# The first stage of a two-layer hybrid encoder kernel: modulation blocks and norm tiles in a fixed order, state-space parameters and weight splits on the vector engine

## The chip, the cores and the metric

The kernel runs on one core of a Trainium2 chip. The metric is the device time of the whole program in microseconds, as the median of several executions. A core has a matrix engine (TensorE, PE in the profile), a vector engine (DVE), a scalar engine for activations and copies (ACT), GpSimd (POOL), and SyncE (SP), which issues most of the DMAs. Each runs its own queue of instructions in order, and semaphores tie the queues together. PEld is PE's loading of weights, which overlaps its matmuls.

## The reference

A trunk of two residual layers on x of 512 positions by 1024 channels, conditioned by a vector c. Only the first layer's mixer (layer 0) bears on the change:

```python
mod = (silu(c) @ ada_w[layer] + ada_b[layer])            # 6 x 1024
sh1, sc1, g1, sh2, sc2, g2 = split(mod, 6)
u = rms_norm(h, norm_w[layer, 0]) * (1.0 + sc1) + sh1
z = u @ hyb_w_in[e]                                      # 1024 -> 512 + 512 + 128 + 128
y_s5  = s5_mixer(z_s5, ...)                              # complex diagonal scan, both directions
y_att = axial_gqa(z_q, z_k, z_v, ...)                    # 8 query heads, 2 key heads, RMS norm and rotary
mix = concatenate([y_s5, y_att]) @ hyb_w_out[e]
h = h + g1 * mix                                         # then a squared-ReLU MLP, then layer 1
```

The state-space mixer turns its parameters into a magnitude exp(lr dt), an angle li dt with its sine and cosine, and complex factors f = (abar - 1) / lambda that scale its input matrices. These *parameters* are 128 x 32 numbers, worked on by many small operations. In the attention q and k are divided by the root mean square of each head, rotated, and q is scaled by 1/8 before the softmax.

## The kernel before

Matrix products run in three passes: each operand is split in a high and a low half (`wh`, `wl` for weights, `acta`, `actb` for activations), and `mm3_tok` adds high by high, low weight by high activation, and high weight by low activation. `split` (L504) makes a weight's halves: ACT copies the high half (L509), another engine subtracts it for the low half (L510).

`hybrid` (the program of the first layer, from L1100 on) runs in this order:

1. *First stage.* Eight tiles of x (128 channels x 512 positions) are loaded. `s5_params` makes the state-space parameters on POOL, through the class `Tiny`, which makes one scalar-tensor-tensor operation out of two of POOL's. `rope_tables` makes the four rotary tables `rcq`, `rsq`, `rck`, `rsk` on POOL. `rstd_bc` squares the x tiles on ACT, adds them on DVE, sums over the partitions on PE (L752), takes the reciprocal root on DVE (L731 to L736, result `nry`), broadcasts it on PE (L756) and copies it to SBUF on ACT (L757). The modulation of 1024 channels comes in four blocks of 256: `ada_load` fetches eight pieces of 128 x 512 and `ada_block` multiplies them by silu(c) and adds them on DVE (L712, L714), sums over the partitions on PE (L716) and adds the bias on DVE (L719, L720). Each block serves two of the eight tiles of x, called a pair here. `norm_tile` makes the normalised, modulated tile: DVE L763, ACT L766 (high half), DVE L767 (low half). PE then multiplies it with the q, k and v columns of the input weight (256 columns of k and v for each of four position blocks, 512 of q: L596 to L598). For k < 3 the low half of the weight tile is made by POOL, after that by DVE.
2. *State-space input and attention preparation.* `s5_tables` (L298 to L304) makes sine and cosine tables, `s5_in` the state-space columns of the projection for two halves, `s5_prep` (L342 to L346) and `s5_lag` (L415) the matrices of one unit of the loop: `PREP` puts preparation 2 on DVE and the others on POOL. `attn_kv` and `attn_q` take the sums of squares by head (`head_ss`: one ACT operation for each head), the reciprocal roots, and the rotation (two products from PSUM on DVE, an addition on POOL). POOL scales the queries (L942) and takes their low halves. The first gate accumulations of `ada_half` (L670, 128 x 512 pieces fetched by ACT's queue into two buffers `nt`) follow on DVE.
3. *The loop.* Eight units of the state-space mixer: phases, the products L441 to L443, the scans L448 on DVE, between them steps of the attention (row maximum on DVE, exponential on ACT, products on PE), and the preparations of later units.
4. *The tail.* Once the last scan is done, the GELU (L1047), the gate, the output projection, the MLP and the second layer follow. PE's order in them is written out by hand; they are the same lines before and after.

What sets the order on an engine is the tile framework's scheduler, which takes instructions as their operands become ready by its reckoning; `issue_after(i)` keeps what stands in its block behind instruction i, and `manual_schedule` fixes PE's order in the tail. Tiles come from pools with a number of buffers for each name: a new tile waits for the readers of the one that it replaces. `weights(wctx, 3, 3, 768)` gives the weight tiles of the first stage three buffers for the raw weight and three for the halves.

## Time and profile before

| | |
|---|---|
| three runs | 1259.51, 1261.17, 1262.28 us, median 1261.17 |
| the profiled execution | 1262.24 us, of which the span of the trace is 1260.4 |
| mean granted clock of PE | 0.973 |
| busy in the span | PE 1174.1 us (93%), PEld 997.9 (79%), DVE 820.2 (65%), ACT 527.5 (42%), POOL 244.9 (19%) |
| the chain of work that ended last | PE 71%, DVE 15%, POOL 8%, issue 3%, ACT 3% |

Times in a trace count from the start of the span. The rows below cut the span at points of the program. At 27.4 PE's first matmul of a norm tile starts; at 42.5 the second operand that it needed is there; at 73.2 DVE ends the norm steps of the fourth pair; at 118.5 DVE begins to feed the loop's first products; at 250.3 the last scan is over. An engine's busy time in a stretch is set against the length of the stretch. PEclk is the TensorE clock granted in the stretch, as a share of 2.4 GHz, so 0.50 is 1.2 GHz. In the timeline a row can stand for several instructions (xcount) from its start on; in square brackets is how long the engine sat idle before, and what released it. Of a single line the duration is given as smallest, median and largest of its instructions.

### The profile page before, as it was taken

The numbers are of one execution on the slowest core, as the hardware profiler recorded it, in microseconds if no ns is written. First come the engines' busy times: TensorE is split into PE (matmuls) and PEld (weight loads), VectorE is DVE, ScalarE is ACT, GpSimd is POOL, SyncE is SP. The second block draws the span as 40 slices with busy tenths as digits, with TensorE's granted clock in tenths as the row PEclk, the third lists the DMA queues.
The fourth block names the chain that finished last, engine by engine and source line by source line (L and its number), as shares of the span: only waits on it lengthen the run. The fifth ranks groups of instructions, "written<-read, shape, count | busy, mean of one in ns | idle before, by whom it ended". The sixth has DMA issues, their size and how long they took to land.

```text
span 1260.4 us, 17174 instructions
## 1 busy us (share of the span) xinstructions
PE 1174.1 (93%) x6552; PEld 997.9 (79%) x6552; DVE 820.2 (65%) x1246; ACT 527.5 (42%) x954; POOL 244.9 (19%) x342
## 2 busy tenths in 40 slices
PE   3678889989999999999999999789999999999997
PEld 2568668777998888888888988569988888888887
DVE  6558999977789875678533779995753322445143
ACT  3147658545352342134422449853543321334130
POOL 9996987520000000000000053000000000000000
PEclk9989889999999999999999999789999999999998
DMA  9421311054538855667332332112242333222311
GB/s 335 129 59 56 88 43 34 2 180 156 200 103 272 274 187 200 216 196 244 112 100 84 101 109 76 50 57 78 69 126 91 101 101 100 91 93 101 101 34 67
DMA packets 83858, 151.76 MB, mean 120 GB/s; under 512 B 5696, under 2 KB 30272, under 8 KB 83776
## 3 DMA queue, kind: packets, MB, share of 16 engines
q1 hardware_dynamic: 75712, 137.04, 33.4%
q10 hardware_dynamic: 8064, 13.64, 3.4%
q8 instruction: 51, 0.84, 0.3%
q14 instruction: 31, 0.25, 0.1%
HBM read 148.55 MB, written 2.10 MB: 120 GB/s over the span
## 4 chain that ended last, share of the span: by engine, by line
PE 71%; DVE 15%; POOL 8%; issue 3%; ACT 3%; DMA 0%; DVEq 0%; ACTq 0%; POOLq 0%
PE ps L557 12%; PE ps L558 12%; PE ps L556 12%; PE px L556 8%; PE px L557 8%; PE px L558 8%; DVE actb L448 2%; DVE wl L510 2%; PE po L984 1%; POOL tiny L77 1%; DVE actb L443 1%; DVE s5m L442 1%; DVE actb L441 1%; DVE nb L966 1%; DVE ti L1404 1%
## 5 line engine op out<-in xcount | busy, mean ns | idle before, releaser
L510 DVE TENSOR_TENSOR wl<-wr,wh 128x1024 fp32r<-128x1024 f32 (+2 forms) x175 | 211.3, 1209 | 288.5 <-ACT wh L509 277.9
L509 ACT CAST wh<-wr 128x1024 fp32r<-128x1024 f32 (+2 forms) x170 | 173.3, 1023 | 437.3 <-PE ps L557 203.6
L557 PE MATMUL ps<-actb,wh 128*128 128x512 f32 (+1 forms) x512 | 181.1, 354 | 0.1
L556 PE MATMUL ps<-acta,wh 128*128 128x512 f32 (+1 forms) x328 | 116.5, 356 | 0.0
L558 PE MATMUL ps<-acta,wl 128*128 128x512 f32 (+1 forms) x328 | 115.9, 354 | 0.0
L556 PE MATMUL ps<-hid,wh 128*128 128x512 f32 x288 | 112.1, 389 | 0.0
L558 PE MATMUL ps<-hid,wl 128*128 128x512 f32 x288 | 112.0, 389 | 0.0
L557 PE MATMUL ps<-hid,wh 128*128 128x512 f32 x288 | 112.0, 389 | 0.0
L557 PEld LDWEIGHTS ps<-actb,wh 128*128 128x128 f32 x512 | 97.5, 190 | 13.5 <-DVE actb L846 0.3
L556 PE MATMUL px<-hid,wh 128*128 128x512 f32 (+1 forms) x288 | 98.9, 343 | 0.0
L557 PE MATMUL px<-hid,wh 128*128 128x512 f32 (+1 forms) x288 | 98.4, 342 | 0.0
L558 PE MATMUL px<-hid,wl 128*128 128x512 f32 (+1 forms) x288 | 98.4, 342 | 0.0
L557 PE MATMUL px<-actb,wh 128*128 128x512 f32 (+1 forms) x224 | 85.5, 382 | 0.0
L638 DVE SCALAR_TENSOR_TENSOR acc<-wr,cact,acc 128x1024 f32<-128x1024 f32 x49 | 62.9, 1284 | 18.7 <-DMA wr<-ada_w 18.3
L556 PEld LDWEIGHTS ps<-acta,wh 128*128 128x128 f32 x328 | 62.7, 191 | 8.5
L558 PEld LDWEIGHTS ps<-acta,wl 128*128 128x128 f32 x328 | 62.6, 191 | 8.4
L1331 POOL MEMSET xp<- 128x2 f32 x8 | 0.7, 98 | 351.6 <-PE px L558 347.3
L556 PE MATMUL ps<-actc,wh 128*128 128x512 f32 (+1 forms) x184 | 65.1, 354 | 0.0
L558 PE MATMUL ps<-actc,wl 128*128 128x512 f32 (+1 forms) x184 | 64.8, 352 | 0.0
L556 PEld LDWEIGHTS ps<-hid,wh 128*128 128x128 f32 x288 | 54.1, 188 | 11.3
L558 PEld LDWEIGHTS ps<-hid,wl 128*128 128x128 f32 x288 | 54.1, 188 | 11.2
L557 PEld LDWEIGHTS ps<-hid,wh 128*128 128x128 f32 x288 | 54.1, 188 | 11.1
(495 smaller groups left out, 2758.4 us busy)
## 6 DMA issues: line engine op xcount, KB each, us to landing
wr<-w SPq DMA_DIRECT2D x128, 512.0 KB, 3.7
wr<-ada_w SPq DMA_DIRECT2D x56, 512.0 KB, 4.5
wr<-wout SPq DMA_DIRECT2D x16, 512.0 KB, 3.5
araw<-ada_w ACTq DMA_DIRECT2D x32, 256.0 KB, 3.4
wr<-win SPq DMA_DIRECT2D x16, 512.0 KB, 3.9
acta<-ada_w SPq DMA_DIRECT2D x16, 256.0 KB, 5.4
actb<-ada_w SPq DMA_DIRECT2D x16, 256.0 KB, 5.4
nt<-ada_w ACTq DMA_DIRECT2D x16, 256.0 KB, 2.8
```

The lines of the kernel that those rows point to most:

```text
L77: self.eng.tensor_scalar(t, a, s, None, op0=op0)
L441: V.tensor_tensor(v[:, xs, dst], er[:, xs], p1[:, :, src], op=ALU.mult)
L442: V.tensor_tensor(m, ei[:, xs], p2[:, :, src], op=ALU.mult)
L443: V.tensor_tensor(v[:, xs, dst], v[:, xs, dst], m, op=op)
L448: self.scan = V.tensor_tensor_scan(vv, m4, vv, 0.0, op0=ALU.mult, op1=ALU.add)
L509: nc.scalar.copy(hi, src)
L510: (lo_eng or nc.vector).tensor_tensor(lo, src, hi.bitcast(F32), op=ALU.subtract)
L556: mm(out, wh, xh, start=first and a == a0 and lead(o), stop=False, skip_group_check=True)
L557: mm(out, wh, xl, start=False, stop=False, skip_group_check=True)
L558: mm(out, wl, xh, start=False, stop=last and a == a0 + kk - 1, skip_group_check=True)
L638: nc.vector.scalar_tensor_tensor(acc, raw, self.ca[:, k:k + 1], acc, op0=ALU.mult, op1=ALU.add)
L966: nc.vector.reduce_max(nb, s, axis=AX.X, negate=True)
```

## The change

The class `Tiny` goes, and the parameter operations of `s5_params` run on the vector engine. The function becomes a generator with two parts: the first, up to the magnitude exp(lr dt), stands ahead of `rstd_bc` in the program, the second is issued behind the last norm tile, together with the rope tables, which also go to the vector engine, and `s5_tables`.

All low halves of weights in the first stage are made by the vector engine. The weight tiles of the stage have four raw buffers in place of three. `ada_load` puts the pieces of blocks 0 and 1 in the activation buffers as before, those of block 2 in the buffers that later hold the rotated queries (`qr0` to `qr3`), those of block 3 in the buffers of the keys and of two attention tiles. Each modulation block, and the splits of the two weight tiles that go with it, are held behind the low halves (and for the splits also the high half) of the pair of norm tiles before. In block 0 the four odd pieces are not accumulated on DVE but multiplied by silu(c) on PE, four one-column matmuls each (L714 of the new kernel). All four blocks write to one PSUM bank. `rstd_bc` returns the broadcast in PSUM, without the copy to SBUF.

`head_ss` takes one ACT operation for the squares of all heads and one sum over them on DVE. The scale of the queries is no longer multiplied into them: POOL's four products go, and the softmax's exponential takes the scale of its rows as its own, with a scaled row maximum from one more one-column ACT operation for each of the 32 steps.

```diff
@@ s5_params
-        V = D = Tiny(self, tp, nc.gpsimd)
+        V = D = nc.vector
...
         reduce(r, t("rn"))
+        mag = pexp(x)
+        yield
...
-        mag = pexp(x)
...
+        yield
@@ wtile
-    def wtile(self, src, pool=None):
+    def wtile(self, src, pool=None, after=()):
...
-        self.split(hi, lo, raw, self.hi_eng, self.lo_eng)
+        with self.behind(*after):
+            self.split(hi, lo, raw, self.hi_eng, self.lo_eng)
@@ ada_load
-            raw = self.tl(self.ap, "actb" if k % 2 else "acta", [P, 2, 256], bufs=8)
+            if cb < 2:
+                raw = self.tl(self.ap, "actb" if k % 2 else "acta", [P, 2, 256], bufs=8)
+            elif cb == 2:
+                if k % 2 == 0:
+                    pair = hp.tile([P, 4, 256], F32, tag=f"qr{k // 2}", name=f"raw{k // 2}")
+                raw = pair[:, k % 2 * 2:k % 2 * 2 + 2]
+            elif k < 4:
+                raw = hp.tile([P, 2, 256], F32, tag=("kth0", "ktl0", "kth1", "ktl1")[k], name=f"rawk{k}")
+            else:
+                raw = self.tl(qp, ("pts", "q2")[k % 2], [P, 2, 256], bufs=2)
@@ ada_block
+            if k in direct:
+                for i in range(4):
+                    nc.tensor.matmul(ps[:, i:i + 1], flat[k][:, i * P:(i + 1) * P], self.ca[:, k:k + 1],
+                                     start=k == direct[0] and i == 0, stop=False, skip_group_check=True)
+            elif k == 0:
-            nc.tensor.matmul(ps[:, i:i + 1], acc[:, i * P:(i + 1) * P], self.ones, start=True, stop=True)
+            nc.tensor.matmul(ps[:, i:i + 1], acc[:, i * P:(i + 1) * P], self.ones, start=not direct and i == 0, stop=True, skip_group_check=True)
@@ rstd_bc
-        nc.scalar.copy(acc, bc)
-        return acc
+        return bc
@@ rope_tables
-                nc.gpsimd.tensor_tensor(o, self.col[tab].rearrange("p (t d) -> p t d", t=4),
+                nc.vector.tensor_tensor(o, self.col[tab].rearrange("p (t d) -> p t d", t=4),
@@ head_ss
-        for h in range(nh):
-            self.nc.scalar.activation(sq, ps[:, h * 64:(h + 1) * 64], AF.Square, accum_out=dst[:, h:h + 1])
+        self.nc.scalar.activation(sq, ps, AF.Square)
+        self.nc.vector.reduce_sum(dst, sq.rearrange("p (h d) -> p h d", h=nh), axis=AX.X)
@@ attn_q
-            nc.gpsimd.tensor_tensor(o[:, :, 0], o[:, :, 0], rq[:, t * 8:t * 8 + 8].unsqueeze(2).to_broadcast([P, 8, 64]), op=ALU.mult)
@@ the softmax step
-        self.exp = nc.scalar.activation(p, s, AF.Exp, bias=nb, accum_out=self.esum[:, h, t:t + 1])
+        r = self.rq[:, t * 8 + h:t * 8 + h + 1]
+        nc.scalar.activation(nb, nb, AF.Identity, scale=r)
+        self.exp = nc.scalar.activation(p, s, AF.Exp, bias=nb, scale=r, accum_out=self.esum[:, h, t:t + 1])
@@ hybrid
-        self.weights(wctx, 3, 3, 768)
+        self.weights(wctx, 4, 3, 768)
...
-        raws = [self.ada_load(aw, 0)]
-        self.lo_eng = nc.gpsimd
-        self.s5_params(sp, tp)
-        self.rope_tables(self.pool(wctx, "rope"))
-        xbc = self.rstd_bc(x, "ps")
+        raws = self.ada_load(aw, 0, hp, qp)
+        params = self.s5_params(sp, tp)
+        next(params)
...
+            cb, a = k // 2, k % 2
+            if a == 0:
+                with self.tc.issue_after(self.last.ins) if k else ExitStack():
+                    mods.append(self.ada_block(qp, raws, cb, psm[:, cb * 4:cb * 4 + 4], (1, 3, 5, 7) if cb == 0 else ()))
+                w += [self.wtile(win[i * P:(i + 1) * P, 512:1280], after=(self.last, self.last_hi) if k else ()) for i in (k, k + 1)]
+                if cb < 3:
+                    raws = self.ada_load(aw, cb + 1, hp, qp)
...
         with self.tc.issue_after(self.last.ins):
+            next(params)
+            self.rope_tables(self.pool(wctx, "rope"))
             self.s5_tables(sp, 0)
```

What stands where on the engines' queues changes in three places. The first is PE's opening, from the sum of the squares on. `ps<-ones,nacc` is that sum, `consts_sb,nry` the broadcast of the root, `ones,pexp` the end of a modulation block, and `wh`, `wl` with `acta`, `actb` the products of norm tiles. Before:

```order
L752 MATMUL ps_371<-ones,nacc_348 128x1 x4
L716 MATMUL p_95_397<-ones,pexp_398 128x1 x4
L756 MATMUL ps_385<-consts_sb,nry_377 128x128 x4
L596 MATMUL ps_395<-wh_448,acta_455 128x256
L596 MATMUL ps_396<-wh_448,acta_455 128x256
L596 MATMUL ps_391<-wh_448,acta_455 128x512
L596 MATMUL ps_392<-wh_448,acta_455 128x512
L596 MATMUL ps_393<-wh_448,acta_455 128x512
L596 MATMUL ps_394<-wh_448,acta_455 128x512
L716 MATMUL p_106_430<-ones,pexp_431 128x1 x4
L597 MATMUL ps_395<-wl_449,acta_455 128x256
L598 MATMUL ps_395<-wh_448,actb_456 128x256
```

After:

```order
L757 MATMUL ps_241<-ones,nacc_218 128x1 x4
L761 MATMUL p_49_255<-consts_sb,nry_247 128x128 x4
L714 MATMUL p_36_217<-cact,actb_150 128x1 x4
L714 MATMUL p_36_217<-cact,actb_154 128x1 x4
L714 MATMUL p_36_217<-cact,actb_158 128x1 x4
L714 MATMUL p_36_217<-cact,actb_162 128x1 x4
L721 MATMUL p_36_217<-ones,pexp_266 128x1 x4
L588 MATMUL ps_264<-wh_295,acta_324 128x256
L589 MATMUL ps_264<-wl_296,acta_324 128x256
L588 MATMUL ps_265<-wh_295,acta_324 128x256
L589 MATMUL ps_265<-wl_296,acta_324 128x256
L588 MATMUL ps_260<-wh_295,acta_324 128x512
```

The group of the second modulation block (`pexp_431`) stood among the first tile's products and now stands behind both tiles of its pair; the sixteen direct products of block 0 stand behind the broadcast of the root, and the first low-half products follow each high one at once.

The second is DVE's queue around the last pair of norm tiles. `modb` is the modulation, `nt` the normalised tile, `wl` the low half of a weight, the `sm_`, `s5mt`, `s5pi` and `s5npr` tiles are parameters, `s5si` and `s5co` the tables of `s5_tables`. Before:

```order
L720 SCALAR_TENSOR_TENSOR modb_154_654<-modb_154_654,cols_sb 128x2
L763 SCALAR_TENSOR_TENSOR nt_735<-h_144,modb_154_654,nacc_348 128x512
L763 SCALAR_TENSOR_TENSOR nt_771<-h_146,modb_154_654,nacc_348 128x512
L767 SCALAR_TENSOR_TENSOR actb_738<-nt_735,modb_154_654,acta_737 128x512
L767 SCALAR_TENSOR_TENSOR actb_774<-nt_771,modb_154_654,acta_773 128x512
L298 SCALAR_TENSOR_TENSOR s5si_802<-sm_phi_204,consts_sb 128x512 x2
L510 TENSOR_TENSOR wl_767<-wr_765,wh_766 128x768
L302 TENSOR_SCALAR s5co_801<-s5si_802 128x1024
L303 SCALAR_TENSOR_TENSOR s5si_802<-s5co_801,s5si_802 128x1024
L304 SCALAR_TENSOR_TENSOR s5co_801<-s5si_802 128x1024
```

After:

```order
L767 SCALAR_TENSOR_TENSOR nt_614<-h_144,modb_111_599,p_49_255 128x512
L767 SCALAR_TENSOR_TENSOR nt_644<-h_146,modb_111_599,p_49_255 128x512
L771 SCALAR_TENSOR_TENSOR actb_617<-nt_614,modb_111_599,acta_616 128x512
L771 SCALAR_TENSOR_TENSOR actb_647<-nt_644,modb_111_599,acta_646 128x512
L212 TENSOR_TENSOR s5pi_676<-sm_phi_188,consts_sb 128x80 x2
L215 MEMSET s5mt_674 128x160
L220 TENSOR_TENSOR sm_m_129_694<-pexp_34_200 128x32
L241 TENSOR_TENSOR sm_den_715<-sm_lr_164 128x32
L242 TENSOR_TENSOR sm_ta_716<-cols_sb 128x32
L884 TENSOR_TENSOR rcq<-consts_sb,cols_sb 128x256
L884 TENSOR_TENSOR rsq<-consts_sb,cols_sb 128x256
L884 TENSOR_TENSOR rck<-consts_sb,cols_sb 128x256
```

The tables of `s5_tables` and the low halves for the state-space columns followed the norm tiles at once; now the second part of the parameters and the rope tables stand between, and the tables come behind them.

The third is POOL's queue where the first two preparations stand. `sm_` tiles are parameters again, `s5cv`, `s5vr`, `s5vi` and `s5ptmp` belong to `s5_prep`, `qr` is a rotated query and `actb` a buffer of the loop's products. Before:

```order
L342 TENSOR_TENSOR s5cv_206_958<-s5pr_220,s5par_946 128x320
L342 TENSOR_TENSOR s5cv_207_959<-s5npr_222,s5par_946 128x320
L256 TENSOR_SCALAR sm_nr_301<-sm_ar_295 128x32
L262 TENSOR_TENSOR sm_ta_303<-sm_ai_296,cols_sb 128x32
L265 TENSOR_TENSOR sm_fi_305<-sm_ai_296,sm_lr_164 128x32
L261 TENSOR_TENSOR sm_fr_304<-sm_nr_301,sm_lr_164 128x32
L263 TENSOR_TENSOR sm_fr_304<-sm_fr_304,sm_ta_303 128x32
L264 TENSOR_TENSOR sm_fr_304<-sm_fr_304,sm_den_302 128x32
```

After:

```order
L390 TENSOR_TENSOR s5dd_952<-consts_sb,cols_sb 128x256
L1220 TENSOR_TENSOR sel<-consts_sb 128x32
L327 TENSOR_TENSOR s5cv_169_918<-s5pr_675,s5par_906 128x320
L327 TENSOR_TENSOR s5cv_170_919<-s5npr_677,s5par_906 128x320
L898 TENSOR_TENSOR qr_1083<-qr_1083,tmp_1084 128x8x64
L943 TENSOR_TENSOR qr_1083<-qr_1083 128x8x64
L898 TENSOR_TENSOR qr_1093<-qr_1093,tmp_1094 128x8x64
L898 TENSOR_TENSOR qr_1103<-qr_1103,tmp_1104 128x8x64
L943 TENSOR_TENSOR qr_1093<-qr_1093 128x8x64
L414 MEMSET actb_1353 128x4
L414 MEMSET actb_1354 128x4
L445 MEMSET actb_1400 128x4
```

POOL went from the parameters to the preparations; now nothing of the parameters stands on it, and the preparations' other operations (`s5vr`, `s5vi`, `s5ptmp`) stand behind the first rotations of the queries and fillings of the loop's buffers, a few rows further on.

## Rows read from the trace of the kernel before

**Rows 1.** Busy time of each engine by stretch, with granted clock and DMA.

```profile
0.00:42.50 42.50, 9.65 (x38) 8.80 (x38) 27.66 (x51) 13.52 (x20) 38.58 (x70) 1.00 0.69 248
42.50:73.20 30.70, 24.84 (x126) 22.04 (x127) 17.53 (x29) 9.61 (x23) 27.97 (x48) 0.83 0.47 150
73.20:118.50 45.30, 41.65 (x311) 37.56 (x310) 32.12 (x69) 29.27 (x129) 34.43 (x47) 0.96 0.20 57
118.50:250.30 131.80, 118.23 (x970) 96.61 (x969) 126.78 (x238) 81.64 (x185) 100.94 (x129) 0.94 0.15 44
250.30:1260.40 1010.10, 979.77 (x5114) 832.88 (x5113) 616.12 (x863) 393.50 (x597) 42.93 (x51) 0.98 0.39 127
```

**Rows 2.** PE's waits up to 300 us: us in total, times, longest.

```profile
PE ps L597 <- POOL wl L510: 11.1, 1, 11.1
```

**Rows 3.** Timeline: start, us, engine, line, operation, tiles, count, idle before.

```profile
21.15 0.20 DVE L736 SCALAR_TENSOR_TENSOR nry<-nra,nry 128x4 f32<-128x4 f32 x1
...
23.01 2.06 PE L756 MATMUL ps<-consts_sb,nry 128*128 128x128 f32 x8
29.73 1.70 PE L716 MATMUL p<-ones,pexp 128*128 128x1 f32 x8
...
32.65 1.39 ACT L766 ACTIVATE acta<-nt,modb 128x512 fp32r<-128x512 f32 x2 [3.20 <-DVE nt L763]
...
60.56 0.94 PE L716 MATMUL p<-ones,pexp 128*128 128x1 f32 x8
67.34 0.58 PE L596 MATMUL ps<-wh,acta 128*128 128x256 f32 x1 [5.83 <-ACT acta L766]
...
78.41 0.28 PE L596 MATMUL ps<-wh,acta 128*128 128x256 f32 x1
...
82.59 0.28 PE L596 MATMUL ps<-wh,acta 128*128 128x256 f32 x1
```

**Rows 4.** Busy time and granted clock of the two microseconds from 71.0.

```profile
71.00:73.00 2.00, 2.00 (x9) 1.81 (x8) 1.87 (x3) 1.36 (x2) 1.92 (x5) 0.50 0.45 130
```

**Rows 5.** Single lines: smallest, median, largest ns; first and last start in us.

```profile
L1513 DVE SCALAR_TENSOR_TENSOR lp_p<-lp_p,lp_w x6: 174/174/176, 453.2 to 454.2; 128x16 f32<-128x16 f32 x6
...
L714 DVE SCALAR_TENSOR_TENSOR pexp<-acta,cact,pexp x12: 741/752/797, 16.2 to 57.9; 128x512 f32<-128x512 f32 x12
...
L448 DVE TENSOR_TENSOR_SCAN actb<-s5m,actb x64: 391/466/1485, 133.1 to 248.8; 128x128 f32<-128x128 f32 x64
...
L670 DVE SCALAR_TENSOR_TENSOR h<-nt,cact,h x14: 721/1150/1723, 119.4 to 178.4; 128x512 f32<-128x512 f32 x14
```

**Rows 6.** DVE's groups up to 262 us: busy us, mean ns, idle before.

```profile
L448 DVE TENSOR_TENSOR_SCAN actb<-s5m,actb 128x128 f32<-128x128 f32 x64 | 42.2, 706 | 0.0
L443 DVE TENSOR_TENSOR actb<-actb,s5m 128x254 f32<-128x254 f32 x32 | 22.3, 718 | 0.0
L442 DVE TENSOR_TENSOR s5m<-s5ei,pb 128x254 f32<-128x254 f32 x32 | 12.9, 403 | 0.0
...
L510 DVE TENSOR_TENSOR wl<-wr,wh 128x768 fp32r<-128x768 f32 x5 | 5.0, 1005 | 6.5 <-ACT wh L509 6.4
```

**Rows 7.** Timeline of ACT, DVE and POOL from 94 to 251 us.

```profile
94.82 1.28 ACT L732 ACT_TABLE_LOAD   x1
...
97.23 0.37 DVE L344 TENSOR_TENSOR s5ptmp<-s5nfpi,s5par 128x256 f32<-128x256 f32 x1
...
117.01 1.63 DVE L415 SCALAR_TENSOR_TENSOR s5dc<-p,consts_sb,s5dc 128x64 f32<-128x64 f32 x4
...
118.03 4.68 POOL L942 TENSOR_TENSOR qr<-qr,rqy 128x512 f32<-128x512 f32 x4
...
125.68 1.60 DVE L670 SCALAR_TENSOR_TENSOR h<-nt,cact,h 128x512 f32<-128x512 f32 x1 [4.87 <-DMA nt<-ada_w]
...
250.19 2.33 DVE L1047 SCALAR_TENSOR_TENSOR nt<-nt,h 128x512 f32<-128x512 f32 x2
```

**Rows 8.** Busy time by engine while POOL runs preparations 0 and 1.

```profile
76.99:96.50 19.51, 17.22 (x100) 15.29 (x100) 8.30 (x15) 10.80 (x40) 19.03 (x26) 0.92 0.21 62
```

More of the change, by code (lines that the diff above doesn't have):

```diff
@@ L513, in wraw, with behind @@
         return self.tl(self.wp, "wr", [P, self.WC], bufs=self.WR)
-    def wtile(self, src, pool=None):
+    def behind(self, *ins):
+        st = ExitStack()
+        for i in ins:
+            st.enter_context(self.tc.issue_after(i.ins))
+        return st
+    def wtile(self, src, pool=None, after=()):
         nk, ncol = src.shape[0] // P, src.shape[1]
@@ L749, in rstd_bc @@
             nc.vector.tensor_tensor(acc, acc, sq, op=ALU.add)
-        ps = self.psum(tag)
+        ps = self.psum(tag[0])
         for t in range(4):
@@ L937, in attn_q @@
             self.qr.append(o)
-        rq = self.rsqrt(hp, ss.rearrange("p t h -> p (t h)"), 32, 64.0, "rq")
-        nc.vector.tensor_scalar(rq, rq, 0.125, None, op0=ALU.mult)
-        for t in range(4):
-            o = self.qr[t]
-            nc.gpsimd.tensor_tensor(o[:, :, 0], o[:, :, 0], rq[:, t * 8:t * 8 + 8].unsqueeze(2).to_broadcast([P, 8, 64]), op=ALU.mult)
             nc.scalar.copy(o[:, :, 1].bitcast(F32R), o[:, :, 0])
             nc.gpsimd.tensor_tensor(o[:, :, 0], o[:, :, 0], o[:, :, 1], op=ALU.subtract)
+        self.rq = self.rsqrt(hp, ss.rearrange("p t h -> p (t h)"), 32, 64.0, "rq")
+        nc.vector.tensor_scalar(self.rq, self.rq, 0.125, None, op0=ALU.mult)
         self.esum = self.tl(hp, "esum", [P, 8, 4])
@@ L1123, in hybrid @@
             x.append(t)
-        raws = [self.ada_load(aw, 0)]
-        self.lo_eng = nc.gpsimd
-        self.s5_params(sp, tp)
-        self.rope_tables(self.pool(wctx, "rope"))
-        xbc = self.rstd_bc(x, "ps")
-        u = []
+        raws = self.ada_load(aw, 0, hp, qp)
+        params = self.s5_params(sp, tp)
+        next(params)
+        u, w, mods = [], [], []
+        psm = self.psum("p5")
+        xbc = self.rstd_bc(x, ("ps", "p5"))
         psq = [self.psum() for _ in range(4)]
         psk = [self.psum() for _ in range(2)]
-        mods = []
-        wt = lambda k: self.wtile(win[k * P:(k + 1) * P, 512:1280])
         for k in range(8):
-            if k % 2 == 0:
-                for cb in range(0 if k == 0 else k // 2 + 1, min(k // 2 + 2, 4)):
-                    if cb:
-                        raws.append(self.ada_load(aw, cb))
-                    mods.append(self.ada_block(qp, raws[cb], cb, self.psum("p5")))
-            m, a = mods[k // 2], k % 2
-            self.lo_eng = nc.gpsimd if k < 3 else None
-            wh, wl = wt(k)
+            cb, a = k // 2, k % 2
[5 more added lines that the diff above has]
+                    raws = self.ada_load(aw, cb + 1, hp, qp)
+            m = mods[cb]
+            wh, wl = w[k]
             xh, xl = self.norm_tile(x[k], xbc, m[:, 2 + a:3 + a], m[:, a:a + 1])
```

30 lines of the change are left out of this document (8 added, 22 removed).

## The prediction

> **What bounds the kernel now.** I read the table by stretches first [rows 1]. VectorE (DVE) is busy 126.78 of the 131.80 us from 118.5 to 250.3, the stretch with the state-space loop, and PE after 250.3 is busy 979.77 of 1010.10. So the kernel is a first part that ends with the last scan on DVE, and a tail in which PE is full. The tail is written in the same order after the change and begins behind that scan: what the change does is how far the scan's end moves. It stands at 250.2, where DVE goes on to the first GELU product [rows 7].
>
> Before 118.5 DVE is not full: busy 27.66, 17.53 and 32.12 in 42.5, 30.7 and 45.3 us, so 41 us idle, and 46 up to 250.3. GpSimd (POOL) is all but full there (38.58, 27.97, 34.43) with the parameter chain [rows 1]. PE stands still 11.1 us for the low half of a weight tile that POOL computes [rows 2]. The change takes these waits away and gives the work to DVE. The question is whether 46 us of DVE idle time shrink by more than DVE's work grows.
>
> **The change part by part, along DVE's queue.**
>
> *Opening.* Of the parameters 39 small operations now stand on DVE ahead of or among the seven additions of the squares and the square-root step. A dependent one of 16 columns takes 0.174 us and they follow every 0.2 (six starts in 1.0) [rows 5], so 7.8 us for 39; about 5 of them fit in before the activations land, and four of block 0's eight products at 0.75 [rows 5] leave. The reciprocal root, finished at 21.35 now [rows 3], I put at 22.8. PE then broadcasts it (2.06) and, in its queue behind that, multiplies half of block 0 directly: 16 matmuls, four times a group like the one of 8 passes that took 1.70 at 29.7 and 0.94 at 60.6 [rows 3], so 3.8 to 6.8, and the last group 0.94 to 1.70. From the end of such a group to the first matmul of a norm tile take 2.0 (the group at 29.73 ends 31.43, the high half of the first tile at 32.65 plus half of 1.39) [rows 3]. First weight matmul: 22.8 + 2.06 + 3.8 + 0.94 + 2.0 = 31.6, up to 35.4; I take 32.5. It starts at 27.4 now but then hangs till 42.5.
>
> *The four pairs.* A tile is 4.18 us of matmuls at full clock (82.59 less 78.41) [rows 3]. Each block's modulation group now stands behind the pair before on PE and the next norm tile waits for it: 8.36 + 0.94 + 2.0 = 11.3 per pair. DVE has seven or eight products (0.68 apart without POOL), two low halves (1.0 each) [rows 5, 6] and four norm steps, 10.3, so PE's chain sets the period. In the 2.0 us PE idles. After 5.83 us idle at 67.3 the granted clock is 0.50, that is 1.2 GHz, until about 73 [rows 3, 4], which costs 2.8 us of a pair. For a gap of 2.0 the price lies between 0 and 2.8; I take 1.0, since the gap is nearer to no gap than to 5.83. Period 12.3 (11.3 to 14.1), so the fourth pair's norm tiles come at 32.5 + 36.9 = 69.4 (65.5 to 77.7). In the trace of before DVE ends the fourth pair at 73.2, where the third stretch begins [rows 1]: nearly nothing is gained for DVE here, because the modulations wait for PE where POOL's split made PE wait before.
>
> *From there to the state-space factors.* DVE does 32.12 us from 73.2 to 118.5 now [rows 1]. Of it two weight halves come earlier and 20 operations of preparation 2 and of the lag blocks (0.27 to 0.66 each, from 97.2 to 118.5 [rows 7]) come later, in all 9.1. Added are the other 43 parameter operations at 0.2 to 0.33 (9.5), four rope tables of 256 columns (1.4, half a product of 512) and eight sums of squares by head (four of 512 columns, four of 128: 3.2); the contended ones get some 2 us shorter as POOL is quiet. 32.1 - 9.1 + 14.1 - 2 = 35. ScalarE (ACT) alternates here between sine and square root, two more table loads at 1.28 [rows 7], for which DVE waits about 2. So the factors and the query scale are ready 1.5 + 35 + 2 = 38.5 after the fourth pair, at 107.9. Now POOL is done with both preparations by 96.5 [rows 8].
>
> *The gate accumulations.* DVE's next rows are the products of the early gate blocks. They read two buffers that ACT's queue refills, and ACT now has phase copies, exponentials and preparation copies ahead of the refills. One such wait was 4.87 [rows 7]. There are about ten refills in this stretch; I take 8 us of waits, bounds 5 and 12.
>
> *The loop.* 126.8 of work now, plus the 20 operations (7.4) and three more attention maxima that come ahead of the last scan (2.4): 136.6. Beside it POOL now has preparations 0 and 1, which DVE did not feel before: POOL was busy 19.03 of 19.51 us in 77.0 to 96.5, of which all but the last factor products (1.5) are theirs, 17.5 [rows 8]; the query scaling of 4.68 [rows 7] is gone: +13. What POOL costs DVE shows in the same operation at different times: a scan 0.391 at best and 0.706 in the mean, 64 times; a sum of two SBUF tiles 0.718 where the product of the same width from PSUM takes 0.403, 32 times; a gate product 0.721 and 1.150, 14 times [rows 5, 6]. That is 20.2 + 10.1 + 6.0 = 36 us of lengthening beside 100.94 us of POOL [rows 1], 0.36 per us. For +13 it gives 4.8, bounds 0 (the operations fall beside PSUM reads) and 13 (every one in DVE's way).
>
> **Sum.** 69.4 + 38.5 + 8 + 136.6 + 4.8 = 257.3 against 250.2: 7.1 later. The profiled execution took 1262.24, 1.07 above the median, so 1261.17 + 7.1 = 1268.3. All edits of lower cost go with this: the rooted norm read from PSUM instead of a copy saves an ACT step of 0.6 on the opening (in the 22.8), the query scale inside the exponential adds 32 one-column ACT steps, hidden under ACT's 81.64 of 131.80 [rows 1]; without that cover they would be some 7 us.
>
> **The rivals.**
> *Slower still.* POOL and DVE exclude each other whole in the loop: +13 instead of 4.8, and the clock falls in every gap (period 14.1, 5.4 more at the fourth pair). 1268.3 + 8.2 + 5.4 = 1282; with the first alone 1276.5. For it speaks that a scan's longest is as long as a POOL operation (1.485) [rows 5], against it the median of 0.466.
> The Trainium skill, "SBUF — State Buffer", section "Who interferes with whom", calls the port pair of the two engines an exclusive lock that one of them holds for its instruction; taken strictly that is this rival's 1276.5, and by the mean of the scans, under twice the best one, the trace bears it out in part.
>
> *Faster.* The lengthening in the loop falls instead of growing: POOL starts the loop with preparations while DVE works on accumulations, maxima from PSUM and waits, and has the four scalings less. If the 36 us fall to 20, the sum loses 4.8 + 16 and the time is 1247.5. It decides from a fall to 28 on (1268.3 - 4.8 - 8 = 1255.5). For it: attention is ready earlier (POOL begins to scale the queries at 118.03 now [rows 7], and by the sum the scale is there at 107.9 and nothing is multiplied) so DVE has more PSUM work to put beside POOL. Against it: POOL has more, not less, in that stretch.
>
> *No change.* The early idle time is worth just what the added work costs: waits of 5 for the accumulations, the clock stays up (3.0 less at the fourth pair), nothing added by POOL: 1268.3 - 3 - 3 - 4.8 = 1257.5 at its lowest; with half of this 1263.
>
> **How the numbers follow.** A measurement tells 0.2%, 2.5 us, from no change: 1258.7 to 1263.7 is the same. Forecast (1263.7 to 1274) 0.42; slower still 0.16; no change 0.14; faster 0.28. Predicted 1268. At the low end the faster rival is let in to 1248, short of its full price; at the high end the slower one to 1285. Outside stays about 0.15. Faster 0.28, same 0.14, slower 0.58; the forecast's own range is 1260 to 1278.
>
> **What would show it.** In the profile after: the first weight matmul at 31 to 36 and no halt for a low half; the fourth pair's last norm step on DVE at 67 to 79; the factors on DVE at 103 to 117; waits of DVE for the gate loads of 5 to 12 in all; DVE over 95% busy from there; scans of 0.7 or more in the mean; the first GELU product at 253 to 262. I am wrong in the pairs if the period is under 11, in the budget if the factors are ready before 100, in the contention if the scans' mean is under 0.6, and wholly if the first GELU product comes before 248.

## The result and the profile after

The changed kernel takes 1272.38 us (median of four runs, 1270.6 to 1275.75) against 1261.41 for the kernel before in the same runs; the ratio is 1.0093 with a 95% interval of 1.008 to 1.0106. It is 11 us slower. The prediction was 1268, slower, with 1263.7 to 1274 for the forecast case.

The profiled execution of the changed kernel took 1275.75 us, 3.4 above its median, with a span of 1273.9, so its trace ends later than the median execution would. Its busy time by stretch follows (PE, PEld, DVE, ACT, POOL, granted clock, DMA share, GB/s). The cuts are the first matmul of a norm tile, the end of the fourth pair's norm steps on DVE, the first gate accumulation, and the end of the last scan; the last row is the whole stretch up to there.

```profile
0.00:31.40 31.40, 12.27 (x56) 12.09 (x56) 17.81 (x66) 10.32 (x16) 6.92 (x16) 1.00 0.99 359
31.40:73.80 42.40, 36.72 (x192) 32.01 (x193) 33.22 (x51) 10.08 (x14) 0.00 (x0) 0.92 0.34 111
73.80:113.30 39.50, 32.94 (x252) 31.23 (x251) 34.39 (x102) 22.95 (x58) 13.15 (x17) 0.91 0.12 34
113.30:264.20 150.90, 123.77 (x1008) 100.47 (x1006) 136.01 (x262) 98.40 (x235) 111.01 (x146) 0.92 0.13 41
0.00:264.20 264.20, 205.68 (x1503) 175.80 (x1503) 221.42 (x479) 141.76 (x320) 131.07 (x178) 0.93 0.27 89
```

The same last row of the kernel before, up to its last scan:

```profile
0.00:250.30 250.30, 194.37 (x1440) 165.01 (x1441) 204.10 (x384) 134.03 (x357) 201.93 (x291) 0.94 0.29 94
```

These two rows are the shortest account of the result. Before, DVE worked 204.1 us and stood idle 46.2 until the last scan was over. Now it works 221.4 and stands idle 42.8. The change gave DVE 17.3 us of work, and only 3.4 of it went into idle time. Behind the scan nothing moved: 1262.24 less 250.3 is 1011.9, and 1275.75 less 264.2 is 1011.6.

Where DVE's idle time of the first stage lies shows in its timeline (start, duration, line, operation, tiles, shapes, count, idle before and what ended it), here the opening of the changed kernel:

```profile
18.82 0.16 DVE L741 SCALAR_TENSOR_TENSOR nry<-nra,nry 128x4 f32<-128x4 f32 x1
18.90 1.83 DVE L495 TENSOR_TENSOR wl<-wr,wh 128x768 fp32r<-128x768 f32 x2
29.48 0.16 DVE L724 TENSOR_TENSOR modb<-p,cols_sb 128x4 f32<-128x4 f32 x1 [8.75 <-PE p L721]
...
29.87 1.41 DVE L767 SCALAR_TENSOR_TENSOR nt<-h,modb,p 128x512 f32<-128x512 f32 x2
```

The root is there at 18.98, then DVE makes two low halves and stands 8.75 us, because its next instruction wants block 0, which PE is multiplying, and the products of block 1 are held behind the first pair. On PE the same time and the pairs that follow read:

```profile
20.91 6.83 PE L714 MATMUL p<-cact,actb 128*128 128x1 f32 x32
27.59 1.84 PE L721 MATMUL p<-ones,pexp 128*128 128x1 f32 x8
31.43 0.58 PE L588 MATMUL ps<-wh,acta 128*128 128x256 f32 x1 [1.99 <-ACT acta L770]
...
42.02 0.95 PE L721 MATMUL p<-ones,pexp 128*128 128x1 f32 x8
44.96 0.39 PE L588 MATMUL ps<-wh,acta 128*128 128x256 f32 x1 [1.99 <-ACT acta L770]
...
59.01 0.39 PE L588 MATMUL ps<-wh,acta 128*128 128x256 f32 x1 [1.99 <-ACT acta L770]
```

The direct products take 6.83 us. The halts of 11.1 and 5.83 us for POOL and ACT [rows 2, 3] are gone, but each of the first three pairs begins with a gap of 1.99 behind the block's group, and pairs follow every 13.5 to 14. (Before the fourth, PE has state-space columns to multiply.)

DVE's waits in the loop are now these (line, what it waited for, us in total, times, longest):

```profile
DVE h L662 <- DMA nt<-ada_w: 7.5, 6, 2.1
DVE mod L680 <- PE p L675: 3.9, 1, 3.9
DVE s5dc L394 <- PE p L385: 1.7, 1, 1.7
```

The three operations of [rows 5, 6] read in the groups of the changed kernel's loop (count | busy us, mean ns of one | idle time before them):

```profile
L433 DVE TENSOR_TENSOR_SCAN actb<-s5m,actb 128x128 f32<-128x128 f32 x64 | 43.5, 728 | 0.0
L428 DVE TENSOR_TENSOR actb<-actb,s5m 128x254 f32<-128x254 f32 x32 | 20.6, 666 | 0.0
...
L662 DVE SCALAR_TENSOR_TENSOR h<-nt,cact,h 128x512 f32<-128x512 f32 x14 | 13.0, 930 | 7.6 <-DMA nt<-ada_w 7.5
...
L427 DVE TENSOR_TENSOR s5m<-s5ei,pb 128x254 f32<-128x254 f32 x32 | 12.9, 403 | 0.0
```

The last line is a product from PSUM, which is as long as before [rows 6].

### The profile page after: what moved, and what is told of

The parts are those of the page before. It is cut to its first block, busy times and chain, and to the rows that moved or that the text cites. A ratio compares the mean times of both kernels' runs of the same rounds, so it can differ in the third digit from the quotient of the medians.

```text
span 1273.9 us, 17144 instructions
## 1 busy us (share of the span) xinstructions
PE 1182.9 (93%) x6584; PEld 1005.2 (79%) x6584; DVE 836.2 (66%) x1337; ACT 534.0 (42%) x915; POOL 173.9 (14%) x229
## 4 chain that ended last, share of the span: by engine, by line
PE 66%; DVE 21%; DMA 5%; issue 4%; ACT 3%; ACTq 0%; POOL 0%; DVEq 0%; POOLq 0%
PE ps L549 10%; PE ps L550 10%; PE ps L548 10%; PE px L548 7%; PE px L550 7%; PE px L549 7%; DMA wr<-ada_w 3%; DVE wl L495 3%; DVE actb L433 2%; DMA wr<-w 1%; PE po L988 1%; DVE acc L630 1%; DVE actb L428 1%; PE ps L588 1%; PE ps L589 1%
## 5 line engine op out<-in xcount | busy, mean ns | idle before, releaser
L548 PEld LDWEIGHTS ps<-hid,wh 128*128 128x128 f32 x288 | 54.1, 188 | 11.1
L549 PEld LDWEIGHTS px<-hid,wh 128*128 128x128 f32 x288 | 54.6, 189 | 6.3
```

The costliest lines, as they stand in the source:

```text
L548: mm(out, wh, xh, start=first and a == a0 and lead(o), stop=False, skip_group_check=True)
L549: mm(out, wh, xl, start=False, stop=False, skip_group_check=True)
```

## The experiments

The theory (A) going in was that of the prediction: the end of the last scan is the sum of what stands on DVE's queue and of DVE's waits. Its rivals were that the fixed order costs, wherever the parameters are worked on (B), and that POOL's preparations, moved into the loop, cost DVE (C). The table gives for each kernel the ratio to the kernel before, and from its profile DVE's busy and idle time up to the end of the last scan. Each profile is of one execution, and that of the changed kernel is 3.4 us above its median, so differences of the last three columns from its row can be 3 us off where the medians are not. "Holds" are the two orders of the change: a modulation block, and the splits of a weight, behind the pair before.

| kernel | median us | ratio (95%) | last scan ends | DVE busy | DVE idle |
|---|---|---|---|---|---|
| before | 1261.2 | 1 | 250.3 | 204.1 | 46.2 |
| changed | 1272.4 | 1.0093 (1.008 to 1.0106) | 264.2 | 221.4 | 42.8 |
| changed, both holds off | 1258.7 | 0.9978 (0.9964 to 0.9992) | 247.4 | 227.7 | 19.7 |
| changed, split hold off | 1274.4 | 1.0106 (1.009 to 1.0121) | 264.1 | 221.7 | 42.4 |
| changed, no direct products | 1267.6 | 1.0055 (1.0041 to 1.0069) | 256.5 | 223.9 | 32.6 |
| changed, parameters on POOL, all early | 1274.3 | 1.011 (1.0097 to 1.0124) | 261.6 | 210.6 | 51.0 |
| changed, parameters on POOL, second part late | 1266.9 | 1.0041 (1.0028 to 1.0055) | 254.4 | 215.1 | 39.3 |
| before, parameters on DVE | 1261.5 | 1.0004 (0.9995 to 1.0013) | 251.1 | 229.2 | 21.9 |
| changed, head sums on ACT | 1268.4 | 1.0063 (1.0051 to 1.0076) | 257.7 | 225.5 | 32.2 |
| changed, query scale on POOL | 1280.3 | 1.0157 (1.0141 to 1.0173) | 269.3 | 223.7 | 45.6 |
| before, query scale in the exponential | 1270.4 | 1.007 (1.0056 to 1.0083) | 259.2 | 203.7 | 55.5 |
| holds off, head sums on ACT | 1259.8 | 1.0 (0.9991 to 1.0008) | 248.4 | 222.6 | 25.8 |
| holds off, head sums on ACT, no direct products | 1264.6 | 1.0035 (1.0023 to 1.0048) | 255.5 | 229.7 | 25.8 |
| holds off, query scale on POOL | 1265.1 | 1.0037 (1.0024 to 1.0049) | 253.5 | 219.8 | 33.7 |

### The holds

The edit takes both holds away; `e6_hold_off`:

```
-                with self.tc.issue_after(self.last.ins) if k else ExitStack():
+                with ExitStack():
...
-                w += [self.wtile(win[i * P:(i + 1) * P, 512:1280], after=(self.last, self.last_hi) if k else ()) for i in (k, k + 1)]
+                w += [self.wtile(win[i * P:(i + 1) * P, 512:1280], after=()) for i in (k, k + 1)]
```

> The changed kernel without the holds: modulation blocks and splits are ordered by the scheduler again (own buffers, direct products and all else stay). In the changed kernel a pair takes 13.5 us, of which DVE works 10.5 and PE 11.5. Theory A (the fixed order costs: the block's group on PE waits for the pair ahead): pairs come every 10 to 11 us, the fourth 6 to 9 us earlier, time 1264 to 1268. Rival (without the hold the accumulations of later blocks stand ahead of the norm steps on DVE and the first tiles come later): the fourth pair within 2 us of 70.9 and the time 1270 to 1275.

It came out at 1258.7, beyond theory A's own 1264 to 1268 and faster than both kernels. Its timeline of DVE in the opening, where the changed kernel stands 8.75 us:

```profile
18.82 0.16 DVE L741 SCALAR_TENSOR_TENSOR nry<-nra,nry 128x4 f32<-128x4 f32 x1
18.90 0.96 DVE L495 TENSOR_TENSOR wl<-wr,wh 128x768 fp32r<-128x768 f32 x1
19.78 0.48 DVE L717 TENSOR_SCALAR pexp<-acta,cact 128x512 f32<-128x512 f32 x1
...
29.48 0.16 DVE L724 TENSOR_TENSOR modb<-p,cols_sb 128x4 f32<-128x4 f32 x1 [1.70 <-PE p L721]
...
57.07 1.42 DVE L771 SCALAR_TENSOR_TENSOR actb<-nt,modb,acta 128x512 fp32r<-128x512 f32 x2
58.40 0.39 DVE L212 TENSOR_TENSOR s5pi<-sm_phi,consts_sb 128x80 f32<-128x80 f32 x2
```

Block 1 is accumulated while PE multiplies block 0, and the norm steps of all pairs are over at 58.4 instead of 73.8. The four pairs' stretch (32.0 to 58.4) and the stretch from there to the first gate accumulation, by engine:

```profile
32.00:58.40 26.40, 24.71 (x124) 21.55 (x125) 22.76 (x38) 8.05 (x11) 0.00 (x0) 0.89 0.43 145
58.40:101.20 42.80, 41.38 (x316) 38.90 (x315) 37.89 (x104) 21.61 (x59) 17.33 (x23) 0.99 0.15 44
...
0.00:247.40 247.40, 202.71 (x1486) 173.44 (x1486) 227.69 (x478) 137.62 (x314) 133.42 (x178) 0.92 0.28 95
```

PE is busy 24.7 of 26.4 us there. DVE works as much as in the changed kernel and 6 us more, and idles 19.7 us in place of 42.8. So the rest of the change does fill DVE's idle time; the fixed order hands it back. The whole gain over the kernel before is small, 0.2%, and clear of the noise by little.

Which of the two holds does it, `e25_split_free` asked:

```
-                w += [self.wtile(win[i * P:(i + 1) * P, 512:1280], after=(self.last, self.last_hi) if k else ()) for i in (k, k + 1)]
+                w += [self.wtile(win[i * P:(i + 1) * P, 512:1280], after=()) for i in (k, k + 1)]
```

> The changed kernel with one of its two holds: the modulation blocks stay held behind the pair before, the weight splits are free. (Without both holds the last norm steps came 15.4 us earlier and the time was 1258.7.) Theory A2 (the hold of the blocks is the cost: DVE stands idle 8.75 us in the opening while eight products of block 1 could run, and each block's group on PE waits for the pair ahead): the period stays near 13, the fourth norm steps at 68 to 71, the time at 1268 to 1273. Rival (the splits held behind the norm steps are what delays a pair's first matmul): the fourth pair under 62 and the time under 1262.

1274.4, and the fourth pair's norm steps start at 71.05. Here is the row of the changed kernel, and behind it that of this one:

```profile
70.92 1.41 DVE L767 SCALAR_TENSOR_TENSOR nt<-h,modb,p 128x512 f32<-128x512 f32 x2
...
71.05 1.41 DVE L767 SCALAR_TENSOR_TENSOR nt<-h,modb,p 128x512 f32<-128x512 f32 x2
```

With the blocks' hold alone the whole loss is there. A kernel with only the splits held was not run, so it is not shown that the splits' hold by itself would be free.

### The direct products

`e2_no_direct`:

```
-                    mods.append(self.ada_block(qp, raws, cb, psm[:, cb * 4:cb * 4 + 4], (1, 3, 5, 7) if cb == 0 else ()))
+                    mods.append(self.ada_block(qp, raws, cb, psm[:, cb * 4:cb * 4 + 4], ()))
```

> The changed kernel with block 0 accumulated whole on DVE (no direct products on PE). In the trace of the changed kernel the direct group takes 6.83 us on PE from 20.91 while DVE idles 8.75 us. Theory A: four more products (3.0 us) end on DVE at about 24 instead, the first weight matmul comes at 28 in place of 31.4, every pair 3.4 us earlier, the last scan 2 to 3.4 earlier: time 1269 to 1270.5. Rival: the later stages wait for something else (gate loads, PE), and the time does not move (1272).

1267.6, 4.8 less than the changed kernel's median and more than theory A expected. The first matmul of a norm tile starts at 26.62 in place of 31.43, the fourth pair's norm steps at 65.06 in place of 70.92:

```profile
26.62 0.58 PE L588 MATMUL ps<-wh,acta 128*128 128x256 f32 x1 [1.99 <-ACT acta L770]
...
65.06 1.41 DVE L767 SCALAR_TENSOR_TENSOR nt<-h,modb,p 128x512 f32<-128x512 f32 x2
```

While block 1 is held, most of PE's 6.83 us is delay: with the four products on DVE the broadcast of the root starts 2.0 later (21.06 in place of 19.04), and the first matmul still comes 4.8 earlier.

### The parameters

In `e1_params_pool` both parts are on POOL and at the start:

```
+class Tiny: ...
-        V = D = nc.vector
+        V = D = Tiny(self, tp, nc.gpsimd)
...
         next(params)
+        next(params)
```

> The changed kernel with all parameter operations back on POOL, both parts of them at the program's start; the weights' low halves, the rope tables, the fixed order and all else stay as changed. Theory A (the time is what stands on DVE's queue up to the last scan): DVE loses the 43 operations behind the fourth pair (9.5 us) and the two waits for sine and table loads (4.9), and POOL makes preparations 0 and 1 ahead of the loop: the last scan ends 14 to 21 us earlier than 264.2, at 243 to 250, time 1251 to 1260. Rival B (the fixed order with its period of 13.5 us per pair is what costs, wherever the parameters stand): the fourth pair stays at 72 and the time above 1268. Rival C (POOL's preparations moved into the loop cost DVE): only the contention comes back, 5 to 7 us, time about 1266.

1274.3, against theory A. It relieved DVE of 10.8 us of work and gave it 8.2 of idle time: one parameter operation that stays on DVE, and ACT's copies of parameters, stood in those queues among the pairs and waited for POOL. DVE's waits up to 270 us in that kernel:

```profile
DVE wl L512 <- ACT wh L511: 10.2, 4, 6.6
DVE s5npr L214 <- POOL s5pi L210: 8.3, 1, 8.3
```

The fourth pair came at 86.5. So this run did not measure the parameters on DVE; it showed how a slow chain on POOL stops other engines through their queues, the way ACT's 7.49 us came about in the kernel before, and behind them PE's 5.83 [rows 3]:

```profile
62.87 0.32 ACT L234 COPY s5mt<-pexp 128x16 f32<-128x16 f32 x2 [7.49 <-POOL pexp L187]
```

`e8_params_late` keeps the second part where the change has it, without the second `next`:

> The changed kernel with the parameters on POOL but in the change's two places: the first part at the start, the second held behind the last norm tile. (With both parts at the start, in the run before this one, DVE and ACT stood 8.3 and 6.6 us for POOL within the pairs, so that run did not tell the parameters' cost on DVE.) Theory A: the pairs stay at 13.5 us, the fourth norm steps at 70 to 71; DVE is rid of 9.5 us behind them, while the POOL chain of 43 operations of 0.25 to 1.1 us takes 25 to 30 us from 74, so the factors are ready at 100 to 105 in place of 112.5: last scan 6 to 10 us earlier, time 1262 to 1267. Rival (POOL's chain beside DVE's work, and behind it both preparations, ends later than the one on DVE): factors after 110, time 1272 or more.

1266.9, at the upper end of theory A's 1262 to 1267: DVE is rid of 6.3 us and the scan ends 9.8 earlier. The mechanism was half right: POOL's factors were ready at 94.1, earlier than the 100 to 105 expected, but the query scale only at 117.2.

`e5_before_dve` is the counter-test, the parameters on DVE in the order of before:

```
-        V = D = Tiny(self, tp, nc.gpsimd)
+        V = D = nc.vector
```

> The kernel before with one part of the change alone: the parameter operations on DVE, without any hold behind the norm tiles (POOL keeps the low halves of the first three weight tiles and the rope tables). In the trace before, PE halts 11.1 us for a low half that POOL makes behind the parameters, and ACT idles 7.49 us at 62.9 for a POOL parameter, so that PE halts 5.8 more. Theory A1 (POOL's slow chain holds ACT's and PE's queues; the 82 operations cost DVE 17 us of which most fits in its 41 us of early idle time): both halts go, the fourth pair comes 8 to 15 us earlier, the time falls by 4 to 10, to 1251 to 1257. Rival B1 (each operation that moves to DVE costs its duration at the end): 10 to 15 slower, 1271 to 1276.

Neither: 1261.5, no change. The table has why: DVE's work grew by 25.1 us and its idle time fell by 24.3. Where DVE may take the operations when it is free, the move pays for itself, and here nothing was left over. The halts of 11.1 and 5.83 us did go, as theory A1 said, but the pairs came no earlier: DVE, busy 67.4 of the first 73.2 us, now had too much ahead of them. The first norm steps started at 37.54 in place of 25.87, the fourth pair's ended at 77.0 in place of 73.2, and PE waited for a block's products instead:

```profile
PE p L716 <- DVE pexp L714: 15.9, 3, 7.7
```

### The head sums

`e3_head_act`:

```
-        sq = self.tl(hp, "tmp", [P, 512], bufs=3)[:, 0:nh * 64]
-        self.nc.scalar.activation(sq, ps, AF.Square)
-        self.nc.vector.reduce_sum(dst, sq.rearrange("p (h d) -> p h d", h=nh), axis=AX.X)
+        sq = self.tl(hp, "hsq", [P, 64], bufs=2)
+        for h in range(nh):
+            self.nc.scalar.activation(sq, ps[:, h * 64:(h + 1) * 64], AF.Square, accum_out=dst[:, h:h + 1])
```

> The changed kernel with the sums of squares by head made by ACT again (one accumulating operation per head) in place of one square and a DVE sum. Theory A: DVE loses 3.7 us (4 sums of 0.674 and 4 of 0.279) in a stretch where it is busy 35.3 of 40.4 us: the time falls by 2 to 3.7, to 1269 to 1270.5. Rival D (ACT's queue with its table loads is the bound there): 40 accumulating steps on ACT delay the roots, and the time rises by 2 to 4, to 1275.

1268.4, the number that theory A named, but not by its reason: DVE's busy time did not fall (225.5 against 221.4), its idle time fell by 10.6. What went was waiting. These two waits of the changed kernel, for the root of the keys and for the sine, both behind ACT's table loads (1.28 us each), are not among this kernel's:

```profile
DVE rky L738 <- ACT rky L737: 3.3, 1, 3.3
DVE s5pi L231 <- ACT s5pi L199: 1.6, 1, 1.6
```

The waits for the gate loads fell as well, from 7.5 us to 3.1, the 3.9 for a modulation's group is gone, and a new wait of 2.1 for ACT came. Why the later waits fell was not looked into. With the holds off, `e22_free_head` (the edits of `e6_hold_off` and `e3_head_act` together):

> The changed kernel without both holds and with the sums of squares by head on ACT; the direct products stay. Theory A: DVE is rid of 3.7 us: 1254 to 1256. Rival (ACT's 40 accumulating steps now stand on the way, since the heads' sums come when ACT makes sines and splits): 1258 or more.

1259.8, no gain over 1258.7 and outside theory A's 1254 to 1256; DVE works 5.1 us less and idles 6.1 more.

### The query scale

`e4_fold_off` takes the scale out of the exponential and back to POOL:

```
...
-        r = self.rq[:, t * 8 + h:t * 8 + h + 1]
-        nc.scalar.activation(nb, nb, AF.Identity, scale=r)
-        self.exp = nc.scalar.activation(p, s, AF.Exp, bias=nb, scale=r, accum_out=...)
+        self.exp = nc.scalar.activation(p, s, AF.Exp, bias=nb, accum_out=...)
...
+            nc.gpsimd.tensor_tensor(o[:, :, 0], o[:, :, 0], rq[...], op=ALU.mult)
```

> The changed kernel with the query scale multiplied in by POOL again (four products) and no scale in the exponential (32 one-column ACT steps less). Theory A: nothing leaves DVE's queue and 4.7 us more of POOL work stand beside it, and the attention's first maxima come some 5 us later: 0 to 2 us slower, 1272 to 1274. Rival E (the 32 added ACT steps lie on the way of the softmax and cost): the time falls by 3 to 7, to 1265 to 1269.

1280.3: this part is worth 8 us in the changed kernel. The prediction had counted it only as 4.68 us less of POOL's work, 1.7 us by its rate. The scans lengthen to 47.3 us in all, and the gate accumulations wait 13.3 us in eleven places:

```profile
L433 DVE TENSOR_TENSOR_SCAN actb<-s5m,actb 128x128 f32<-128x128 f32 x64 | 47.3, 791 | 0.0
...
L662 DVE SCALAR_TENSOR_TENSOR h<-nt,cact,h 128x512 f32<-128x512 f32 x14 | 14.4, 1027 | 13.3 <-DMA nt<-ada_w 13.3
```

The same part alone in the kernel before, `e10_before_fold` (the edit the other way round):

> The kernel before with one other part alone: the query scale inside the exponential (POOL's four products go, 32 one-column ACT steps come). Taking this part out of the changed kernel cost 8 us (1280.3 against 1272.4). Theory A: it is worth the same here, since POOL's scaling stands at 118 to 122.7 ahead of the query halves and of the loop's preparations: 4 to 8 us faster, 1253 to 1257. Rival (in the kernel before the preparations 0 and 1 are done by 96, so POOL's four products hold up nothing that the first unit needs): within 0.2%, 1259 to 1263.

1270.4, 9 us slower, outside both expectations. DVE's waits up to 259.2 us in that kernel hold a new one, of the row maxima for the scores:

```profile
DVE nb L964 <- PE pa L962: 7.6, 3, 4.4
```

POOL goes to the low halves of the queries earlier, at 106.5 in place of 125.5, beside DVE's rotations and preparation 2: the query scale is ready at 122.3 in place of 116.3. With the holds off, `e24_free_foldoff` (the edits of `e6_hold_off` and `e4_fold_off` together):

> The changed kernel without both holds and with the query scale multiplied in by POOL again. Undoing the scale in the exponential cost 8 us in the changed kernel, and putting it into the kernel before cost 9. Theory F (its sign goes by whether POOL makes preparations 0 and 1 behind the queries, as in the changed kernel, or has made them before): preparations stand behind the queries here too, so undoing it costs 4 to 8 us: 1263 to 1267. Rival (it depends on how far DVE is behind, and not on POOL's order): within 2 us of 1258.7, or faster.

1265.1, 6.5 slower than with the scale in the exponential. So the part is worth 6.5 to 8 with the rest of the change and costs 9 in the kernel before. That fits the theory that it pays where POOL makes preparations 0 and 1 behind the queries, but three runs that differ in much else do not prove it; the cause of the 9 stays open.

### Together

`e20_free_best` has the three edits that were faster alone, `e6_hold_off`, `e2_no_direct` and `e3_head_act` together (no holds, no direct products, head sums on ACT):

> The changed kernel without both holds, without the direct products and with the sums of squares by head on ACT: the three edits that were each faster alone (by 13.7, 4.8 and 3.9 us). Theory A: the head sums add their 3.9; the direct products' 4.8 came from DVE's idle 8.75 us, which block 1 now fills, so they add only 0 to 2: time 1252 to 1256. If all add up: 1250. Rival (behind the pairs PE and ACT now set the pace, and nothing more is won): 1257 to 1261.

1264.6, slower than the holds off alone and outside all three expectations. The scheduler now puts nearly all accumulations of blocks 1 to 3 ahead of the second pair on DVE, whose norm steps start at 43.06 in place of 35.94 with the direct products kept. PE, short of tiles, is busy 4.7 of the 8 us from 36 to 44; from 49 to 65.4 it is busy 15.6 of 16.4. Behind the third pair DVE goes from low half to low half and waits each time for ACT's high half, and ACT for PE to be done with the weight tile that it replaces:

```profile
52.16 0.96 DVE L495 TENSOR_TENSOR wl<-wr,wh 128x768 fp32r<-128x768 f32 x1 [1.46 <-ACT wh L494]
56.34 0.96 DVE L495 TENSOR_TENSOR wl<-wr,wh 128x768 fp32r<-128x768 f32 x1 [3.21 <-ACT wh L494]
60.52 0.96 DVE L495 TENSOR_TENSOR wl<-wr,wh 128x768 fp32r<-128x768 f32 x1 [3.22 <-ACT wh L494]
64.44 0.69 DVE L495 TENSOR_TENSOR wl<-wr,wh 128x512 fp32r<-128x512 f32 x1 [2.96 <-ACT wh L494]
```

The fourth pair comes at 65.4 instead of 55.5. With the holds the direct products were a loss of 4.8 us; without them, and with the head sums on ACT, they are worth 4.8 (1259.8 against 1264.6), by the order that the scheduler finds with them. Gains of single edits do not add up here.

## Why the prediction was right, point by point

**What bounds.** Right: the tail is the same to 0.3 us, and the time moved by what the last scan moved. DVE, idle 46 us before, was the engine to count on. Of the signs named beforehand the first matmul, the fourth pair, the factors, the gate waits and the scans' mean (0.728) came as said. Two did not: the first GELU product starts at 264.2, later than 253 to 262, and DVE is busy 90% of the last stretch (136.0 of 150.9), not over 95%.

**Opening.** The root came at 18.98 instead of 22.8. Twenty parameter operations, not five, fitted in before the first addition of the squares, which starts at 9.34 where it started at 8.28, and the additions took 0.68 us each in place of 0.88 beside a quieter POOL; the last one ends at 15.3 as before.

```profile
8.28 5.96 DVE L749 TENSOR_TENSOR nacc<-nacc,nt 128x512 f32<-128x512 f32 x6 [2.89 <-ACT nt L748]
...
9.34 0.69 DVE L754 TENSOR_TENSOR nacc<-nacc,nt 128x512 f32<-128x512 f32 x1
```

(The first row is of the kernel before.) The direct group took 6.83 and the last group 1.84, the upper ends of 3.8 to 6.8 and 0.94 to 1.70 and a little over. The two errors cancelled, which was luck: the first matmul at 31.43, predicted 32.5.

**Pairs.** The step was right that the norm tiles wait for their block on PE and that nothing is won for DVE here, and its size was off. The period was 13.5 to 14 instead of 12.3, mostly because a pair's matmuls took 10.59 us (31.43 to 42.02), 10.2 and 10.0 in place of 8.36, so 1.7 to 2.2 more where 1.0 was taken. The bound of 2.8 held it. In the second and third pair the granted clock fell behind the gap (last section). In the first pair the gap is not shown to be the cause: with the holds off only 0.40 us of idle time stood before it, and its matmuls were as slow. The fourth pair's first tile was ready for PE at 72.5 (its norm step at 70.92 plus 1.56, as in the first pair), predicted 69.4.

**To the factors.** 40.9 us after that, predicted 38.5; they were ready at 113.4, within the 103 to 117 named. Two waits on DVE for ACT's alternating tables cost 3.3 and 1.6, where 2 had been taken.

**Gate accumulations.** 7.5 us of waits, predicted 8. But all waits of the stretch come to 14.9: 3.9 for a modulation's group on PE and 1.7 for a lag block were not in the sum.

**Loop.** The contention in this term was mis-sized, and its sign was wrong. The rule of 0.36 us of lengthening per microsecond of POOL would have added 4.8. POOL worked 111.0 us in the stretch instead of 100.9, and the three groups took 43.5, 20.6 and 13.0, in all 77.1, instead of 42.2, 22.3 and 15.6 [rows 5, 6], in all 80.1. DVE was busy 136.0, not 141.4: the contention came out 7.8 lower than summed, the rest of DVE's work 2.4 higher. The rival that the two engines exclude each other whole (13 us) is further off still. A mean of one trace did not carry over. That POOL's price depends on which DVE operations stand beside it fits the rows: the products from PSUM took 0.403 us before and after. But no run varied that alone. (The rate itself had taken the gate products' median, 1.150, for their mean, which is 15.6 over 14, 1.11; that makes 0.5 of the 36 us.) The Trainium skill, "SBUF — State Buffer", section "Who interferes with whom", calls the shared port pair an exclusive lock, but lets only instructions that use the pair contend, so its rule does not ask for the whole 13 us; the 0.403 us agree.

**Sum.** 72.5 + 40.9 + 14.9 + 136.0 = 264.3, against 69.4 + 38.5 + 8 + 141.4 = 257.3. The loop's overestimate of 5.4 hid part of three underestimates (3.1, 2.4 and 6.9). Without it the sum would have been 12.4 short, so that the time lies in the range is in part luck. In the profiled execution the scan's end moved by 13.9 us; against the median the forecast of 7.1 later stands beside 11 measured.

**What the prediction did not see.** It took the order of the blocks as given, and called the pairs neutral because the old order had ended them at the same time. The runs show that the hold on the blocks is enough for the whole loss: with it alone the time is 1274.4, and without both holds the same work ends the pairs 15.4 us earlier and the kernel is 0.2% faster than before. A hint stood in its own arithmetic: it had the root at 22.8 and the first matmul at 32.5, and block 1's products, some six us of work, behind that; DVE had little else to do in between. The edits called of lower cost were not small either: the query scale was worth 8 us.

## What to carry to other kernels

When work moves to another engine, write down that engine's busy and idle time up to the point that decides; the move costs what does not fit into the idle time, and here 25.1 us of added work fitted to within 0.8 as long as the scheduler could place it. A hold that makes an order tidy takes that freedom away, here at 13.7 us: before one is kept, look at what the waiting engine could do in the gap (here eight products of 0.75 in 8.75 us). And undo parts singly, but do not add their gains: three edits that won 13.7, 4.8 and 4 us alone were together slower than the first alone.

## What the runs showed of the hardware

In the second pair of the changed kernel PE had eight one-column passes (0.95 us) and a gap of 2.0 behind it. Its 512-column matmuls first started 0.23 us apart, and from 46.5 on 0.43. The granted clock was 0.50, which is 1.2 GHz, from 46.5 to 48.5, and the same again in the third pair:

```profile
46.50:48.50 2.00, 2.00 (x7) 1.55 (x6) 1.96 (x4) 0.00 (x0) 0.00 (x0) 0.50 0.00 0
...
60.50:62.50 2.00, 2.00 (x6) 1.63 (x5) 1.97 (x4) 0.00 (x0) 0.00 (x0) 0.50 0.00 0
```

The gap of 0.86 before the matmuls at 70.84 was not followed by such a fall: the clock reads 1.00 from 70 to 76. In the first pair 512-column matmuls start 0.43 us apart until 35.86 and 0.23 apart from 39.28 on, the same two paces, while the row of the stretch shows a granted clock of 1.00:

```profile
32.40:35.90 3.50, 3.50 (x11) 2.73 (x10) 3.43 (x6) 0.35 (x1) 0.00 (x0) 1.00 1.07 387
```

The pace of the matmuls and the record of the clock do not agree there; which of the two is off was not settled. With the holds off the first pair has a gap of only 0.40 before it and starts at the same slow pace (512-column matmuls at 32.98, 33.41 and 33.83), so no gap of 2.0 is needed for it:

```profile
31.96 0.58 PE L588 MATMUL ps<-wh,acta 128*128 128x256 f32 x1 [0.40 <-ACT acta L770]
```

One-column matmuls, each with a stationary operand of its own, took long: the sixteen direct products, in 32 passes, took 6.83 us, 0.21 each, as long as nine DVE products of 512 columns. Part of that may be the slow pace of this stretch: the group of eight passes behind them took 1.84 us at 27.59, and the same group 0.95 at 42.02.
